# Two query heads take the first k tile beside the forget heads, and weight blocks are rounded behind chosen Exps

## The chip, the core and the metric

The kernel runs on one core of one Trainium2 chip. The metric is the device time of one execution in microseconds (us). Before the change three timed runs took 719.71 to 720.10 us, median 720.06 us.

Engine names are those of the profile: PE multiplies matrices, ACT does activations and copies, DVE does elementwise work, POOL (GpSimd) here fills constants and issues some transfers, SP only issues transfers. Every engine runs its own instructions strictly in the order in which they stand.

## The reference

One decoder layer over 512 positions of width 1024, in float32. What matters for this change is its beginning: the RMSNorm of x, and one projection whose columns are cut into heads.

```
h = rms_norm(x, norm_mix)
proj = h @ w_in
hq, hf, hi, hg, mq, mk, mv = split(proj, IN_SPLITS)
o_hgrn = hgrn2_mixer(hq, hf, hi, hg, lb, hgrn_norm)      # 4 heads of 128
#   f = lb + (1-lb) sigmoid(hf);  b = cumsum of log f inside chunks of 32
#   q_t = hq exp(b);  k_t = (1-f) exp(-b);  k_end = (1-f) exp(b_last - b)
#   o = causal(q_t k_t^T) hi + state part, then a norm and a gate from hg
o_moba = moba_attention(mq, mk, mv)
x = x + concat(o_hgrn, o_moba) @ w_out
```

Cross-attention into 256 memory tokens, a squared-ReLU MLP and a last RMSNorm follow. The change does not touch them.

## The kernel before

**Products in three parts.** Each float32 operand is split into a rounded high part and the rest (for a weight block: `wh` and `wl`, for x: `xhi` and `xlo`). A product is three matmuls: high by high, high by low, low by high. The high part of a weight block is made by an ACT copy (`split_raw`), the low part by a DVE subtraction right behind it. Blocks are numbered by use: 0 to 3 hold the forget heads (`hf`), 4 to 7 the values (`hi`), 8 to 11 the query heads (`hq`, one head each), 12 to 15 `mv`.

**Loading.** A block arrives in one of three raw buffers (`wr`). The load of block u, issued by SP, waits until the DVE subtraction of block u-3 has read the same buffer. `need(u)` is called before the matmuls of block u: it loads ahead as far as the three buffers allow and splits blocks up to u+2 (`SPLIT_AHEAD`). From block 8 on, each load also takes the next of a list of transfers between tensors in device memory (the tiles `m` and `u`, sums of weights for later stages); POOL issues most of them, and each waits for the matmul that stood last at the previous `need`.

**The first projection.** Four heads `hf` are accumulated over the eight k tiles of x, which arrive one by one. Before the first tile is there PE runs 11 small matmuls on a tile of ones (`warm`). The first block is loaded by heads: heads 0 and 1 and heads 2 and 3 of its first k tile come by two transfers from the ACT queue, the rest by SP. Beside this ACT and DVE sum the squares of x; two matmuls into the tile `nr` add them over partitions, just ahead of the last k tile, and ACT makes `rb` = 1/sqrt by a Ln and an Exp (`rsqrt_of`). Each change of function set costs an `ACT_TABLE_LOAD`.

**Forget gates and what follows.** `ev_f` multiplies each `hf` bank by `rb` (DVE), takes the sigmoid (ACT) and scales it (DVE), all into `Fz`. Then one ACT instruction takes the log of all four heads (`lnf`), and `hgrn_pre` works through the heads: a running sum `b` on DVE, three Exps on ACT (`eb`, `kt`, and the decay, in place in `lnf`), and some twenty DVE instructions that end in `ke`. Meanwhile PE does the values `hi` (`tm_stage`: four banks, four blocks) and then the query heads. When a query head is complete, `ev_q` scales its bank on DVE into `qx` (two halves, each with products by `dc` and `ee`) and `q4`. The attention part of the head, `hgrn_out`, is woven into the matmuls of the next heads: transposes of `ke` (`ket`), then 28 small matmuls into a bank `a` that need `qx`.

**What sets the order.** Up to the last k tile of `hf` the order is the written one. After it a scheduler orders each engine's instructions by its own estimates; the interleaving of side work into the matmul stream goes by a table of costs (`Pace`). All instructions carry the line of the recording helper, 118, so the profile is read by tile names.

## Time and profile before

| what | value |
|---|---|
| timed runs, median of 3 (lowest, highest) | 720.06 us (719.71, 720.10) |
| profiled execution: its span, the only time that its page gives | 717.5 us |
| PE busy | 709.5 us, 99% of the span |
| DVE busy | 580.7 us, 81% |
| ACT busy | 451.8 us, 63% |
| POOL busy | 81.1 us, 11% |
| moved by DMA | 155.58 MB, mean 217 GB/s |

The span runs from the first instruction to the last of one profiled execution. "Busy" is the time in which an engine had work; a busy share near 100% says that the engine bounds the kernel unless its own instructions are stretched. A row of the timeline gives the start and the length of a run of like instructions, and in brackets how long the engine sat idle before them and what released it. Tile names have their buffer numbers left out, so `wh` stands for any rounded weight block.

### The profile page before, as it was taken

Reading aid. Unit: us, or ns where it says so; the run is one execution under the profiler, and the core shown is the slowest. Engines: PE = TensorE matmul, PEld = TensorE weight load, DVE = VectorE, ACT = ScalarE, POOL = GpSimd, SP = SyncE. Lnnn points to the kernel's source line nnn. Section 1 sums busy time; section 2 is a strip of 40 time slices with the busy share of each in tenths; the row PEclk is TensorE's granted clock in tenths of the full one; section 3 lists DMA queues with packets and bytes.
Section 4 is the critical chain, followed back from the end, with each engine's and each line's share of the span. In section 5 each row is a group of like instructions: output and inputs, shape, how many; then the busy total and the mean of one; then the engine's idle time right before and its main releaser. Section 6 shows DMA issues by size and latency. Waiting matters only on the chain.

```text
span 717.5 us, 10748 instructions
## 1 busy us (share of the span) xinstructions
PE 709.5 (99%) x4038; PEld 613.2 (85%) x4038; DVE 580.7 (81%) x882; ACT 451.8 (63%) x654; POOL 81.1 (11%) x98
## 2 busy tenths in 40 slices
PE   9999999999999999999999999999999999999996
PEld 7888888888888888888888999999999888888885
DVE  6899537898787777777578889989899999987886
ACT  7884585546586677656565865566657655546672
POOL 2511132000000000002201111011110100110000
PEclk9999999999999999999999999999999999999999
DMA  8999689975556856458986587886898965998523
GB/s 295 274 281 318 166 175 253 368 257 144 156 173 195 249 175 202 148 177 200 267 266 156 139 225 197 223 206 193 218 233 258 288 220 192 276 276 252 177 89 117
DMA packets 62531, 155.58 MB, mean 217 GB/s; under 512 B 5232, under 2 KB 19184, under 8 KB 61968
## 3 DMA queue, kind: packets, MB, share of 16 engines
q1 hardware_dynamic: 47008, 116.43, 46.3%
q0 software_dynamic: 14592, 37.75, 28.7%
q10 hardware_dynamic: 880, 0.72, 0.3%
q8 instruction: 31, 0.51, 0.3%
q14 instruction: 20, 0.16, 0.1%
HBM read 152.79 MB, written 48.23 MB: 280 GB/s over the span
## 4 chain that ended last, share of the span: by engine, by line
PE 98%; DMA 1%; ACT 0%; DVE 0%; DVEq 0%; SPq 0%; issue 0%; ACTq 0%
PE Y L118 16%; PE X L118 12%; PE xo L118 8%; PE XB L118 6%; PE XA L118 6%; PE mkq L118 6%; PE xq L118 6%; PE wo L118 6%; PE mv L118 3%; PE hg L118 3%; PE hq L118 3%; PE Z L118 3%; PE hf L118 3%; PE memX L118 3%; PE hi L118 3%; PE memY L118 2%
## 5 line engine op out<-in xcount | busy, mean ns | idle before, releaser
L118 DVE TENSOR_TENSOR wl<-wr,wh 128x1024 fp32r<-128x1024 f32 (+2 forms) x139 | 165.6, 1196 | 33.8 <-ACT wh L118 27.1
L118 ACT ACTIVATE wh<-wr 128x1024 fp32r<-128x1024 f32 (+2 forms) x139 | 142.8, 1036 | 75.0 <-PE X L118 16.3
L240 POOL DMA_DIRECT2D u<-in_ws_dram x32 | 27.4, 874 | 320.9 <-PE xt L118 87.7
L118 PE MATMUL X<-op,wh 128*128 128x512 f32 (+1 forms) x264 | 62.9, 385 | 0.0
L118 PEld LDWEIGHTS X<-op,wh 128*128 128x128 f32 x264 | 47.2, 189 | 8.5
L118 PE MATMUL Y<-op,wh 128*128 128x512 f32 x192 | 47.2, 391 | 0.0
L118 PEld LDWEIGHTS Y<-op,wh 128*128 128x128 f32 x192 | 35.0, 189 | 6.6
L118 PEld LDWEIGHTS X<-op,wl 128*128 128x128 f32 x256 | 33.5, 191 | 1.6
L118 PE MATMUL X<-op,wl 128*128 128x256 f32 x256 | 34.1, 282 | 0.0
L118 PE MATMUL Y<-OS,wh 128*128 128x256 f32 x256 | 33.4, 283 | 0.0
L118 PEld LDWEIGHTS Y<-OS,wh 128*128 128x128 f32 x256 | 32.5, 192 | 0.7
L118 DVE TENSOR_TENSOR op<-g,op 128x1024 fp32r<-128x1024 f32 x24 | 29.3, 1219 | 2.8 <-ACT op L118 2.8
L118 ACT ACTIVATE op<-g 128x1024 fp32r<-128x1024 f32 x28 | 29.3, 1045 | 0.6 <-PE XB L118 0.6
L118 ACT ACT_TABLE_LOAD x20 | 25.7, 1283 | 2.2 <-issue 1.8
L118 PEld LDWEIGHTS Y<-op,wl 128*128 128x128 f32 x192 | 25.3, 191 | 1.3
L118 PE MATMUL Y<-op,wl 128*128 128x256 f32 x192 | 25.7, 282 | 0.0
L118 PE MATMUL xq<-x1hi,wl 128*128 128x512 f32 x64 | 25.6, 399 | 0.0
L118 PE MATMUL mkq<-xhi,wh 128*128 128x512 f32 x64 | 25.4, 397 | 0.0
L118 PE MATMUL mkq<-xhi,wl 128*128 128x512 f32 x64 | 25.4, 397 | 0.0
L118 DVE TENSOR_TENSOR wl<-wD,wh 128x1024 fp32r<-128x1024 f32 x15 | 18.4, 1224 | 8.6 <-ACT wh L118 7.9
L118 PE MATMUL xq<-x1hi,wh 128*128 128x512 f32 x64 | 25.3, 396 | 0.0
L118 PE MATMUL mkq<-xlo,wh 128*128 128x512 f32 x64 | 25.2, 394 | 0.0
(370 smaller groups left out, 1914.0 us busy)
## 6 DMA issues: line engine op xcount, KB each, us to landing
wr<-in_ws_dram SPq DMA_DIRECT2D x87, 512.0 KB, 5.0
u<-in_ws_dram POOLq DMA_DIRECT2D x32, 512.0 KB, 6.8
wr<-u SPq DMA_DIRECT2D x32, 512.0 KB, 4.4
u<-in_ws_dram SPq DMA_DIRECT2D x16, 512.0 KB, 11.9
wr<-m SPq DMA_DIRECT2D x16, 512.0 KB, 3.5
m<-in_ws_dram POOLq DMA_DIRECT2D x12, 512.0 KB, 9.8
m<-in_ws_dram POOLq DMA_DIRECT2D x16, 256.0 KB, 6.0
wA<-in_ws_dram SPq DMA_DIRECT2D x8, 512.0 KB, 5.1
```

Source lines behind the costliest of these rows:

```text
L118: return f(*args, **kw)
L240: return nc.gpsimd.dma_start(dst, src, accum_op=ALU.add, max_dma_last_dim=4 * D)
```

## The change

Six things are done.

1. Two query heads (blocks 8 and 9) get their first k tile (128 of 1024 rows) through tiles of their own: one transfer of 128 KB into `qr`, an ACT copy into `qh`, a DVE subtraction into `ql`, and six matmuls right behind those of the four forget heads on k tile 0. Later these two heads start at k tile 1. The number of matmuls stays.
2. `warm` has 8 matmuls and not 11. Heads 2 and 3 of the first weight tile are loaded by SP behind the first x tile, no longer from the ACT queue; `qr` follows them, ahead of the second x tile.
3. The two query banks are taken from the pool `acc` at the start, so the first two banks of `hi` come from the pool of side banks.
4. Weight blocks 5 and 6 are rounded on ACT behind the first Exp of `rsqrt_of`; at k tile 6 `need` splits one block less ahead.
5. Block 12, the first of `mv`, is rounded behind the Exp of the last head's decay; the preparation of the last head (`hgrn_pre`) is drained before the last two query heads.
6. The call order of `ev_f` is heads 2, 0, 1, 3.

```
-    GAP, SLACK, WARM = 4, 2.5, 11
+    GAP, SLACK, WARM = 4, 2.5, 8
...
     def split_raw(u, raw, a, b, eng=None):
-        A.activation(his[u][:, a:b], raw[:, a:b], AF.Copy)
+        rounded = A.activation(his[u][:, a:b], raw[:, a:b], AF.Copy)
+        if u in (5, 6):
+            tc.add_manual_dep(rounded.ins, first_root[0].ins.name, BEHIND)
+        elif u == W_MV:
+            tc.add_manual_dep(rounded.ins, last_decay[0].ins.name, BEHIND)
...
-    def need(u):
+    def need(u, ahead=SPLIT_AHEAD):
...
-        want_load, want_split = min(last, u + LOAD_AHEAD + 1), min(last, u + SPLIT_AHEAD + 1)
+        want_load, want_split = min(last, u + LOAD_AHEAD + 1), min(last, u + ahead + 1)
...
+    W_HQ, QE = 8, 2
+    q_raw, q_hi, q_lo = (s2(d, n)[:, :QE * P] for d, n in ((F32, "qr"), (F32R, "qh"), (F32R, "ql")))
     SY.dma_start(vec, vecs)
     load_x(0)
     load_first(0, 0, slice(0, 2), A)
-    load_first(0, 0, slice(2, 4), A)
+    load_first(0, 0, slice(2, 4))
+    SY.dma_start(q_raw.rearrange("p (n c) -> p n c", n=QE), ws[W_HQ:W_HQ + QE, :, :P].rearrange("n p c -> p n c"))
     load_x(1)
...
     split_first(0, 0, slice(2, 4))
+    A.activation(q_hi, q_raw, AF.Copy)
+    V.tensor_sub(q_lo, q_raw, q_hi.bitcast(F32))
...
-        A.activation(dst, dst, AF.Exp, scale=-0.5)
+        first_root.append(A.activation(dst, dst, AF.Exp, scale=-0.5))
...
+    q_accs = [acc_bank(f"hq{j}") for j in range(QE)]
...
-            need(k // 2)
+            need(k // 2, SPLIT_AHEAD - (k == KT - 2))
...
+        if k == 0:
+            cols = [slice(n * P, (n + 1) * P) for n in range(QE)]
+            for acc, c in zip(q_accs, cols):
+                mm(acc, q_hi[:, c], a_hi, True, False)
+            for acc, c in zip(q_accs, cols):
+                mm(acc, q_lo[:, c], a_hi, False, False)
+            for acc, c in zip(q_accs, cols):
+                mm(acc, q_hi[:, c], a_lo, False, False)
-    for h in range(HEADS):
+    for h in (2, 0, 1, 3):
         ev_f(h, accs[h])
...
-        A.activation(lf, lf, AF.Exp)
+        last_decay[0] = A.activation(lf, lf, AF.Exp)
...
-    tm_stage(u, x_act, 4, ev_hi, "hi")
+    tm_stage(u, x_act, 4, ev_hi, "hi", beside=(0, 1))
...
-    fm_stage(u, x_act, T, ev_q, "hq", ONE * 4)
+    for n in range(QE):
+        need(u + n)
+        for k in range(1, KT):
+            fm_k(u + n, q_accs[n], x_act, k, False, k == KT - 1)
+        ev_q(n, q_accs[n])
+    drain(("pre", HEADS - 1))
+    fm_stage(u + QE, x_act, T, lambda n, acc: ev_q(n + QE, acc), "hq", ONE * (4 - QE))
```

The order of the instructions moves at three places that matter below. The rows name the operation, what it writes and reads with buffer numbers, and the shape.

SP's queue from its start, before:

```order
L118 DMA vec_112<-in_vecs_dram 128x52
L118 DMA xraw0_122<-in_xT_dram 128x512 x2
L118 DMA wr0_130<-in_ws_dram 128x4x128
L118 DMA xraw0_122<-in_xT_dram 128x512
L118 DMA wr1_136<-in_ws_dram 128x4x256
```

And in the change:

```order
L118 DMA vec_112<-in_vecs_dram 128x52
L118 DMA xraw0_122<-in_xT_dram 128x512
L118 DMA wr0_133<-in_ws_dram 128x2x128
L118 DMA qr_128<-in_ws_dram 128x2x128
L118 DMA xraw0_122<-in_xT_dram 128x512
L118 DMA wr0_133<-in_ws_dram 128x4x128
L118 DMA xraw0_122<-in_xT_dram 128x512
```

Two transfers of 128 KB now stand between the first and the second tile of x (`xraw0`); the first of the two came from ACT's queue before.

ACT around the first reciprocal root (`rb1`), before:

```order
L118 ACTIVATE wh4_309<-wr4_255 128x1024
L118 ACTIVATE wh5_339<-wr5_257 128x1024
L118 ACTIVATE wh6_406<-wr6_259 128x1024
L118 ACTIVATE rb1_242<-nr_250,eps_118 128x512
L118 ACT_TABLE_LOAD
L118 ACTIVATE rb1_242<-rb1_242 128x512
L118 ACTIVATE lbv_245<-lbv_245 128x8
L118 ACT_TABLE_LOAD
L118 ACTIVATE Fz_244<-Fz_244 128x512 x4
L118 ACTIVATE wh7_461<-wr7_313 128x1024
L118 ACT_TABLE_LOAD
L118 ACTIVATE lnf_400<-Fz_244 128x2048
```

And in the change:

```order
L118 ACTIVATE wh4_320<-wr4_260 128x1024
L118 ACTIVATE rb1_245<-nr_255,eps_118 128x512
L118 ACT_TABLE_LOAD
L118 ACTIVATE rb1_245<-rb1_245 128x512
L118 ACTIVATE lbv_248<-lbv_248 128x8
L118 ACTIVATE wh5_407<-wr5_262 128x1024
L118 ACT_TABLE_LOAD
L118 ACTIVATE Fz_247<-Fz_247 128x512 x4
L118 ACTIVATE wh6_417<-wr6_264 128x1024
L118 ACTIVATE wh7_472<-wr7_324 128x1024
L118 ACT_TABLE_LOAD
L118 ACTIVATE lnf_401<-Fz_247 128x2048
```

The roundings of blocks 5 and 6 moved from ahead of the root to between it and the log `lnf`; the next rounding, of block 8, stands right behind `lnf` in both.

DVE behind the forget banks, before:

```order
L118 TENSOR_TENSOR Fz_244<-hf3_249,rb1_242 128x512
L118 TENSOR_SCALAR lbv_245<-lbv_245 128x4
L118 TENSOR_TENSOR own_430<-rb1_242,ident_121 128x512
L118 TENSOR_SCALAR Fz_244<-Fz_244,lbv_245 128x512 x4
L118 TENSOR_REDUCE rc1_243<-own_430 128x4
L118 TENSOR_TENSOR wl7_462<-wr7_313,wh7_461 128x1024
```

And in the change:

```order
L118 TENSOR_TENSOR Fz_247<-hf3_252,rb1_245 128x512
L118 TENSOR_SCALAR lbv_248<-lbv_248 128x4
L118 TENSOR_TENSOR wl5_408<-wr5_262,wh5_407 128x1024
L118 TENSOR_SCALAR Fz_247<-Fz_247,lbv_248 128x512 x4
L118 TENSOR_TENSOR wl6_418<-wr6_264,wh6_417 128x1024
L118 TENSOR_TENSOR own_441<-rb1_245,ident_121 128x512
L118 TENSOR_TENSOR wl7_473<-wr7_324,wh7_472 128x1024
```

The subtractions `wl5` and `wl6`, which set free the raw buffers of the loads of blocks 8 and 9, moved behind the products of `hf` with `rb1`. In both programs SP's queue has the loads of blocks 8, 9 and 10 in a row, each waiting for such a subtraction. One more pair of DVE rows changed places: `qx0` of head 1 (`hq1`) now stands between the first product of `qx1` of head 0 and the two that finish it. On PE, apart from the six matmuls and the three of `warm`, nothing moved. POOL's rows stand as before, but the first four transfers into `m0_0` wait for the end of k tile 5 where they waited for that of k tile 3, since the load of block 8 that brings them is written one `need` later.

More of the change, by code (lines that the diff above doesn't have):

```diff
@@ L301, in hybrid_layer @@
     AFTER = mybir.DependencyInfo(mybir.DependencyClass.Sync, mybir.DependencyReason.DATA)
+    BEHIND = mybir.DependencyInfo(mybir.DependencyClass.NoSync, mybir.DependencyReason.SCHED_ONLY)
     marks = [None]
@@ L331, in sums_after @@
         return u % 2 == 0 and (4 <= u - FF2 < 14 or u - FF2 >= 26)
-    held = []
+    W_MV = 12
+    held, first_root, last_decay = [], [], [None]
     def later(f):
@@ L516, in fm_stage, with tm_stage @@
             u += size
-    def tm_stage(u0, act, ntok, evac, name):
-        accs = [acc_bank(f"{name}{t}") for t in range(ntok)]
+    def tm_stage(u0, act, ntok, evac, name, beside=()):
+        accs = [(side_bank if t in beside else acc_bank)(f"{name}{t}") for t in range(ntok)]
         for j in range(4):
@@ L873, in ev_q @@
         start(hgrn_out(h, qx, q4), ("out", h))
-    fm_stage(u, x_act, T, ev_q, "hq", ONE * 4)
+    assert u == W_HQ
+    for n in range(QE):
[5 more added lines that the diff above has]
+    fm_stage(u + QE, x_act, T, lambda n, acc: ev_q(n + QE, acc), "hq", ONE * (4 - QE))
     u += 4
```

## The prediction

> **What bounds the kernel now.** I read the busy shares of the page first:
>
> ```profile
> PE 709.5 (99%) x4038; PEld 613.2 (85%) x4038; DVE 580.7 (81%) x882; ACT 451.8 (63%) x654; POOL 81.1 (11%) x98
> ```
>
> Then all waits of PE (us in total, times, longest):
>
> ```profile
> PE warm L118 <- POOL eps L592: 1.0, 1, 1.0
> PE hf L118 <- ACT xhi L118: 0.3, 1, 0.3
> ```
>
> Then the beginning of the chain of work that ended last (start, us, what), and a window at the end of the span (stretch, width, busy time and count of PE, PEld, DVE, ACT and POOL, granted clock, DMA share, GB/s):
>
> ```profile
> 1.19 3.74 DMA xraw<-in_xT_dram
> 5.57 19.36 PE hf L118 x84
> ```
>
> ```profile
> 710.90:714.20 3.30, 0.00 (x0) 0.00 (x0) 2.04 (x4) 0.97 (x4) 1.41 (x2) 1.00 0.47 170
> ```
>
> PE is busy 99% of the 717.5 us span and waits twice in all, both times before its first `hf` at 5.57. From there it is filled to 710.9, where the last matmul is behind it. This decides how everything below counts. Other engines cost nothing by being busy; a delay anywhere counts only if it opens a gap on PE, and such a gap then passes whole to the end. A gain can come only from an earlier first `hf`, since the matmuls behind it stay the same in number: six of them are only moved forward.
>
> How much earlier it can be, by two rows of the timeline, a window, and two DMA issues with their us to landing:
>
> ```profile
> 0.99 4.29 PE L118 MATMUL warm<-ones 128*128 128x128 f32 x22 [0.99 <-POOL eps L592]
> 5.01 0.51 ACT L118 ACTIVATE xhi<-xraw,vec 128x256 fp32r<-128x256 f32 x1 [1.31 <-DMA xraw<-in_xT_dram]
> ```
>
> ```profile
> 0.99:4.30 3.31, 3.31 (x15) 3.31 (x16) 0.43 (x1) 1.90 (x3) 2.96 (x10) 1.00 0.69 169
> ```
>
> ```profile
> xraw<-in_xT_dram SPq DMA_DIRECT2D x1, 256.0 KB, 3.7
> wr<-in_ws_dram ACTq DMA_DIRECT2D x1, 128.0 KB, 2.5
> ```
>
> The 11 `warm` matmuls are 22 rows; 15 rows took 3.31 us, so 8 matmuls (16 rows) end near 4.5 and leave room for at most 1.0 us. The matmul waits for `xhi`, and `xhi` for the first x tile, which took 3.7 us from its issue at 1.19.
>
> **The change, part by part.**
>
> *Start.* The second transfer of ACT's queue, 128 KB, ran beside the x tile and now follows it. Without any sharing, a tile of 256 KB must take longer than the 2.5 us that 128 KB took; the added 128 KB cost 0.4 us at the 338 GB/s of the window 45:60 that is quoted below (an estimate). So landing lies between 2.9 us (gain 0.8) and 3.7 (no gain). I take 3.1, since the second transfer started last and overlapped only in part: **gain g = 0.6 us**, bounds 0 and 1.0. The six matmuls cost 6 x 0.23 us (19.36/84) = 1.4 us here and save the same later: 0 in the sum. They are also the cover for the 256 KB that now arrive ahead of the second x tile (0.8 us at the same rate, of which half came beside it before; against 1.4 - g = 0.8 us of added PE work). ACT's copy `qh` and DVE's `ql` (128x256 like the `xhi` row, 0.5 us each) lie beside PE's twelve matmuls on tile 0; without that cover they would cost up to 1.0 us.
>
> *The log of the gates comes later.* PE's last matmul into `nr`, and ACT's rows around the first root:
>
> ```profile
> 25.01 0.40 PE L118 MATMUL nr<-nrl,ones_r 128*128 128x512 f32 x1
> ```
>
> ```profile
> 22.98 3.03 ACT L118 ACTIVATE wh<-wr 128x1024 fp32r<-128x1024 f32 x3
> 25.91 0.67 ACT L118 ACTIVATE rb<-nr,eps 128x512 f32<-128x512 f32 x1
> ...
> 32.91 1.06 ACT L118 ACTIVATE wh<-wr 128x1024 fp32r<-128x1024 f32 x1 [0.78 <-DMA wr<-in_ws_dram]
> ...
> 35.29 1.92 ACT L118 ACTIVATE lnf<-Fz 128x2048 f32<-128x2048 f32 x1
> 37.11 1.04 ACT L118 ACTIVATE wh<-wr 128x1024 fp32r<-128x1024 f32 x1
> 38.06 0.61 ACT L118 ACTIVATE Fz<-Fz 128x512 f32<-128x512 f32 x1
> ```
>
> Before, the root's Ln stood behind three roundings, at 25.91. Now two of them are gone from there, but `nr` is later by the six matmuls: 25.41 + 1.4 - 0.6 = 26.2, so the root starts 0.3 later, not earlier. Then `wh5` and `wh6` (one every 0.95 us: 37.11 to 38.06) stand between root and `lnf`: +1.9. The 0.78 us in which ACT waited for block 7 are swallowed: -0.78. Together `lnf` comes **1.4 us later**, at 36.7.
>
> *Where that lag goes.* DVE's rows behind `lnf` and at the end of its chain, a window between them, and the PE row that reads the result:
>
> ```profile
> 45.00:60.00 15.00, 15.00 (x68) 12.40 (x67) 14.99 (x40) 9.42 (x15) 5.95 (x8) 1.00 0.98 338
> ```
>
> ```profile
> 37.31 2.34 DVE L118 TENSOR_TENSOR_SCAN b<-scan_mask,lnf 128x512 f32<-128x512 f32 x2 [1.83 <-ACT lnf L118]
> ...
> 63.54 0.41 DVE L118 TENSOR_TENSOR qx<-hq,eb 128x256 f32<-128x256 f32 x1
> 63.99 0.29 DVE L118 TENSOR_TENSOR qx<-qx,dc 128x128 f32<-128x128 f32 x1
> 64.20 0.22 DVE L118 TENSOR_TENSOR qx<-qx,ee 128x64 f32<-128x64 f32 x1
> ```
>
> ```profile
> 65.93 0.25 PE L118 MATMUL a<-qx,Fz 128*32 128x96 f32 x1
> ```
>
> DVE waits 1.83 us for `lnf`, then works without a gap: 14.99 of 15 us between 45 and 60. A lag at 37 us therefore is still there at 64 us. The second half of `qx` of the first head is finished at 64.42; PE's first matmul that reads it starts at 65.93, so there are 1.5 us of slack. PE is g earlier, DVE 1.4 later, and the moved `qx0` of the next head puts some 0.2 us more (63.54 to 63.99 less what overlaps) ahead of the last two. Stall: 0.6 + 1.4 + 0.2 - 1.5 = **0.7 us**. Bounds: 0, if DVE's small gaps take up the lag or PE reaches `a` later, and 1.2. Since a larger g makes the lag of `lnf` smaller by as much, this stall hardly depends on g.
>
> *Block 8 comes later still.* This is the term that decides the sign. SP's load of block 8 waits for `wl5`. DVE's rows at its old and its new place, three answers on loads of 512 KB with their us to landing (issued around 15, between 24 and 40, and at 35.5 us), a window, and the DMA queues between 37 and 39 us:
>
> ```profile
> 24.06 2.36 DVE L118 TENSOR_TENSOR wl<-wr,wh 128x1024 fp32r<-128x1024 f32 x2 [0.26 <-ACT wh L118]
> ...
> 31.24 0.68 DVE L118 TENSOR_TENSOR own<-rb,ident 128x512 f32<-128x512 f32 x1
> ```
>
> ```profile
> wr<-in_ws_dram SPq DMA_DIRECT2D x1, 512.0 KB, 3.6
> ```
>
> ```profile
> wr<-in_ws_dram SPq DMA_DIRECT2D x4, 512.0 KB, 7.7
> ```
>
> ```profile
> wr<-in_ws_dram SPq DMA_DIRECT2D x1, 512.0 KB, 7.5
> ```
>
> ```profile
> 33.00:39.00 6.00, 6.00 (x28) 4.98 (x27) 4.17 (x6) 5.95 (x6) 2.28 (x2) 1.00 1.12 221
> ```
>
> ```profile
> q0 software_dynamic: 211, 0.40, 109.6%
> ...
> q1 hardware_dynamic: 1, 0.00, 0.5%
> ```
>
> Before, `wl5` was the second of the two rows at 24.06 and ended at 26.4. Now it stands where `own` stood, 31.24 + 0.3, and takes 1.2: it ends near 32.7, and the load is issued 6.3 us later than before. Its rounding `wh8` stands right behind `lnf` on ACT and could start at 37.11 + 1.4 = 38.5. So the load may take 5.8 us. The load around 15 us had SP's queue alone (3.6); the four between 24 and 40 have a median of 7.7; the one issued at 35.5, the nearest in time, took 7.5. Between 33 and 39 us the DMA engines are full (share 1.12) with POOL's transfers in device memory; from 37 to 39 the rows give POOL's queue q0 109.6% and SP's q1 0.5%, although a load was pending. And the stretch gets fuller: of the eight transfers below, POOL issued the first four at 17.09, and these now wait for a later k tile like the others.
>
> ```profile
> 17.09 3.21 POOL L269 DMA_DIRECT2D m<-in_ws_dram  x4 [12.93 <-PE hf L118]
> 22.50 2.94 POOL L269 DMA_DIRECT2D m<-in_ws_dram  x4 [2.20 <-PE hf L118]
> ```
>
> I take 7.5: block 8 lands at 40.2 to 40.3 and `wh8` is **1.8 us late**. Bounds: 0 at 3.6 us of latency, 3.7 at 9.5 us. Behind `wh8` on ACT stand the last gate scaling, a table load and the Exps that DVE's chain needs next, so this lag goes the way of the first, into the wait of `a`: +1.8, with no slack left to take it. Blocks 9 and 10 are issued some 8 and 3 us later too, but their roundings stood at 43.65 and 45.63, which leaves them over 8 us each: 0 by the same latency.
>
> The Trainium skill says in "DMA: Bandwidth & Descriptors", section "Queues, rings and completion order", that each DMA engine goes round robin between the queue rows that have work, packet by packet. By that rule SP's queue gets a share as soon as it has work, and this speaks against the last term. The trace does not agree in the 37 to 39 us window, where q1 had next to nothing.
>
> *The rest.* The order of `ev_f`, block 12 behind the last decay, and the swapped banks move ACT and DVE work between 66 and 85 us that has PE work beside it; PE's waits are unchanged there: 0. The granted clock stays at 1.00 in the 3.3 us after the last matmul (row 710.90), so a stall of 1 to 3 us costs its own length.
>
> **Sum**: -0.6 + 0.7 + 1.8 = **+1.9 us**. The profiled execution would go from 717.5 to 719.4; the median of the timed runs, 720.06, is 2.6 above that span, and I keep that difference: **722.0 us**.
>
> **The rivals.**
>
> *A: block 8 lands in time.* If SP's queue gets its turn among POOL's transfers, the load needs half the full rate, between 3.6 and 5.8 us. This is the round robin just named. Then W = 0 and the sum is -0.6 + 0.7 = +0.1: 720.2 us. For it: all loads between 24 and 40 did land, in 7.5 to 9.5 us, with the engines full. Against it: none was as fast as 5.8.
>
> *B, the other side: PE is not stalled at all, and g survives.* The place is PE's first `a` with the second half of `qx`. If block 8 is in time and DVE regains 0.7 us of its lag, so that this half is ready when PE gets there, only the start is left: 719.4 (719.1 with g = 1.0). For it: DVE gives up `wl5` and `wl6` from its order ahead of the 1.83 us in which it waited for `lnf`, and a scheduler may have left small gaps between 37 and 45 us. Against it: that idle time lay ahead of the chain, not in it, and 14.99 of 15 us leave nothing to regain.
>
> *C: the first `hf` run at the slow pace.* The `warm` rows ran 15 in 3.31 us, then the last 7 in 0.98 us (to 5.28), so PE became faster near 4.3, though the window has the granted clock at 1.00. With `warm` ending at 4.5 and a pause behind it, the pace could fall again; if `hf` loses what `warm` lost (3.31 - 15 x 0.14 = 1.2 us), 723.2. Against it: the 0.3 us pause of before left no trace.
>
> *D: the lag cascades.* Latency 9.5 us and block 9 late too: +3.7 + 0.1 = 723.9.
>
> **How the numbers follow.** A difference of 0.2%, 1.4 us, is about what a measurement of this kernel can tell from no change. Forecast (block 8 late by 0.5 to 3 us) 0.58; A 0.22; B 0.06; C 0.03; D 0.07; and 0.04 for something missed on the faster side, since the start alone can give 1.0 us and not 1.4. Of the forecast 0.40 lies above +1.4 us (a latency of 7.1 us and more), 0.18 below. Slower by over 0.2%: 0.40 + 0.03 + 0.07 = 0.50. Within 0.2%: 0.18 + 0.22 + 0.06 = 0.46. Faster: 0.04. The range reaches from B, 719.3, to 723.5, just below D; the forecast alone would be 720.7 to 723.2.
>
> **What the changed profile would show.** The first `hf` near 5.0 (not 5.57) and `xhi` near 4.4: g. The log `lnf` near 36.7. Block 8's load issued near 32.7, with 7 to 8 us to landing, and ACT idle some 1.8 us before the rounding behind `lnf`, released by a DMA. In PE's waits a new row of about 2.5 us, `a` waiting for `qx` of DVE near 65, and the last matmul near 712.8. If that row is missing, B; if it is 0.7, A. A latency near 4 us, or `lnf` at its old place, would make the prediction wrong, as would a gap on PE anywhere else.

## The result, and the profile after

The changed kernel takes 728.92 us (median of 4 runs, 727.88 to 730.02), the kernel before 719.88 us in the same comparison. The ratio is 1.0128 with a 95% interval of 1.0114 to 1.0142: **9 us slower**. The forecast was 722.0 us, range 719.3 to 723.5. The direction was right and the size was not: the time lies 5.4 us above the range.

The profiled execution has a span of 726.8 us (717.5 before), so 9.3 us are to be found. First the busy shares of its page, and all waits of PE:

```profile
PE 712.0 (98%) x4032; PEld 614.2 (85%) x4032; DVE 581.3 (80%) x883; ACT 452.1 (62%) x655; POOL 81.1 (11%) x98
```

```profile
PE a L118 <- DVE qx L118: 6.5, 1, 6.5
PE warm L118 <- POOL eps L601: 1.0, 1, 1.0
```

One wait of 6.5 us stands where none was. It is the wait that the prediction named (PE's bank `a` for `qx`), but it was to last 2.5 us. The rows around it tell why. DVE between 63 and 73 us, ACT's row at the same time, and one row of the chain of waits:

```profile
63.55 0.42 DVE L118 TENSOR_TENSOR qx<-hq,eb 128x256 f32<-128x256 f32 x1
70.17 1.23 DVE L118 TENSOR_TENSOR wl<-wr,wh 128x1024 fp32r<-128x1024 f32 x1 [6.20 <-ACT wh L118]
71.32 0.29 DVE L118 TENSOR_TENSOR qx<-qx,dc 128x128 f32<-128x128 f32 x1
```

```profile
69.09 1.06 ACT L118 ACTIVATE wh<-wr 128x1024 fp32r<-128x1024 f32 x1 [7.86 <-DMA wr<-in_ws_dram]
```

```profile
51.10 17.88 DMA wr<-in_ws_dram
```

Read them from the bottom. The load of block 12, the first of `mv`, was issued at 51.10 and took 17.9 us. ACT could round it only at 69.09. DVE's subtraction `wl12` waited for that, 6.2 us, and it stands in the middle of the first head's `qx`: ahead of it the first product (63.55), behind it the product with `dc` (71.32) that PE's bank `a` needs.

Before the change the order on DVE was the same. DVE's rows there, the load of block 12 with its us to landing, and PE's first matmul that reads block 12 itself:

```profile
61.40 0.42 DVE L118 TENSOR_TENSOR qx<-hq,eb 128x256 f32<-128x256 f32 x1
61.73 1.21 DVE L118 TENSOR_TENSOR wl<-wr,wh 128x1024 fp32r<-128x1024 f32 x1
62.87 0.28 DVE L118 TENSOR_TENSOR qx<-qx,dc 128x128 f32<-128x128 f32 x1
```

```profile
wr<-in_ws_dram SPq DMA_DIRECT2D x1, 512.0 KB, 8.0
```

```profile
77.75 0.39 PE L118 MATMUL mv<-wh,xhi 128*128 128x512 f32 x1
```

Block 12 was issued at 49.66 then and landed at 57.7, 4 us ahead of its subtraction. PE needs it only for `mv`, some 12 us of its work behind bank `a`; in the change PE stood still because of what was queued behind the block.

The rest of the loss is the clock. Windows of the changed kernel (stretch, width, busy and count of PE, PEld, DVE, ACT, POOL, granted clock, DMA share, GB/s):

```profile
65.00:69.00 4.00, 0.32 (x8) 0.05 (x7) 0.00 (x0) 0.00 (x0) 0.00 (x0) 1.00 0.56 222
69.00:72.00 3.00, 0.21 (x8) 0.21 (x12) 1.83 (x5) 2.49 (x3) 0.00 (x0) 0.61 0.05 22
72.00:76.00 4.00, 3.99 (x53) 2.90 (x47) 4.00 (x14) 0.00 (x0) 0.00 (x0) 0.50 0.80 277
```

After PE had stood idle from 65.3 to 71.8 it worked on at a granted clock of 0.50 (1.2 GHz) until 76: four us of work at half speed. Comparing the start of the same matmuls in both traces gives the whole account: at the end of `hf` the new start had gained 0.5 us; at bank `a` and behind it PE lost 9.2, of which 6.5 are the wait; after that the lag stays at 8.65 us to the last matmul. Another 0.6 us lie behind the last matmul (below, at the stores).

Why was block 12 late? The DMA engines from 20 to 26 and from 26 to 60 us, first before and then after the change:

```profile
20.00:26.00 6.00, 6.00 (x28) 4.92 (x27) 4.80 (x7) 3.56 (x5) 3.25 (x5) 1.00 0.89 289
26.00:60.00 34.00, 34.00 (x152) 28.13 (x151) 31.11 (x86) 27.52 (x39) 10.63 (x12) 1.00 1.01 295
```

```profile
20.00:26.00 6.00, 6.00 (x28) 4.97 (x27) 4.80 (x8) 2.04 (x3) 2.61 (x4) 1.00 0.41 132
26.00:60.00 34.00, 34.00 (x152) 28.09 (x151) 30.25 (x76) 27.86 (x38) 14.16 (x17) 1.00 1.01 284
```

Their share falls from 0.89 to 0.41 there: 0.48 of 6 us, 2.9 us of all engines are not used, since POOL's first four copies now go out at 23.39 and not at 17.09 (e1 below, which has them early again, has 0.88). From 26 to 60 us the engines are full (1.01 in both), so there is no free time in which to catch this up. And the loads of blocks 8 and 9 are themselves issued 6.5 and 8.6 us later than before, because `wl5` and `wl6` moved. Which of the two matters, and how, the experiments had to tell.

### The profile page after: what moved, and what is told of

Read it like the earlier page. It is cut to its first block, busy times and chain, and to the rows that moved or that the text cites. A ratio compares the mean times of both kernels' runs of the same rounds, so it can differ in the third digit from the quotient of the medians.

```text
span 726.8 us, 10736 instructions
## 1 busy us (share of the span) xinstructions
PE 712.0 (98%) x4032; PEld 614.2 (85%) x4032; DVE 581.3 (80%) x883; ACT 452.1 (62%) x655; POOL 81.1 (11%) x98
## 4 chain that ended last, share of the span: by engine, by line
PE 93%; DMA 4%; DVE 2%; ACT 1%; issue 0%; DVEq 0%; POOL 0%; ACTq 0%; POOLq 0%
PE Y L118 16%; PE X L118 12%; PE xo L118 8%; PE XB L118 6%; PE XA L118 6%; PE mkq L118 6%; PE xq L118 6%; PE wo L118 6%; DMA wr<-in_ws_dram 4%; PE mv L118 3%; PE hg L118 3%; PE Z L118 3%; PE memX L118 3%; PE hf L118 3%; PE memY L118 2%; PE xs L118 2%
## 5 line engine op out<-in xcount | busy, mean ns | idle before, releaser
L118 PE MATMUL xq<-x1lo,wh 128*128 128x512 f32 x64 | 25.2, 393 | 0.0
```

Of the source, the lines that this page charges most:

```text
L118: return f(*args, **kw)
```

## The experiments

Times are medians beside the kernel before on the same chip (719.6 to 719.8 us in all of them). "Lag" is how much later than before the change the last matmul stands in the profiled execution; for the changed kernel it is 8.6 us. Kernels in which PE waits for late blocks scatter by 2 to 8 us between executions, and a profile shows one of these, so for them it says more on the mechanism than on the size.

| kernel | median us | ratio to before, 95% | lag us |
|---|---|---|---|
| the change | 728.92 | 1.0128 (1.0114 to 1.0142) | 8.6 |
| e1 copies early again | 725.31 | 1.0078 (1.0061 to 1.0095) | 3.5 |
| e2 copies late alone | 719.59 | 1.0007 (0.9996 to 1.0018) | 1.3 |
| e6 rounding late alone | 720.95 | 1.0016 (1.0007 to 1.0025) | 0.7 |
| e8 only block 6 late | 720.93 | 1.0015 (1.0006 to 1.0023) | 0.5 |
| e7 `m3` copies later | 721.35 | 1.0023 (1.0014 to 1.0033) | 0.5 |
| e3 `wl12` behind `qx` | 727.55 | 1.0106 (1.0077 to 1.0135) | 7.3 |
| e4 block 12 free | 729.96 | 1.0145 (1.0129 to 1.0160) | 8.6 |
| e14 blocks 12, 13 last | 723.79 | 1.0062 (1.0042 to 1.0081) | 2.6 |
| e12 filled, wrong place | 731.03 | 1.0154 (1.0122 to 1.0186) | 7.8 |
| e13 filled ahead of `a` | 726.25 | 1.0092 (1.0076 to 1.0107) | 6.9 |
| e5 start alone | 720.42 | 1.0010 (1.0002 to 1.0019) | 0.6 |
| e10 start without query tile | 721.20 | 1.0024 (1.0015 to 1.0033) | 2.1 |
| e9 one more transfer | 719.93 | 1.0000 (0.9992 to 1.0009) | 0.2 |
| e11 best put together | 719.96 | 1.0007 (0.9998 to 1.0016) | 0.1 |

### Two causes: late copies, late loads

e1 takes the changed kernel and calls the first four copies early again:

```
     def load_unit():
-        for _ in range(sums_after(u)):
+        for _ in range(sums_after(u) if u != W_HQ else 0):
             more_sums()
...
             need(k // 2, SPLIT_AHEAD - (k == KT - 2))
+            if k == KT - 2:
+                more_sums()
+                more_sums()
```

> The changed kernel, with one thing undone: the first four copies of POOL into m0 are again called at k tile 6 and so wait for the end of k tile 3 (they went out at 17.09 us before the change and at 23.39 us after it); the load of block 8 and all rounding stay where the change put them. Theory 1 (the late copies leave the DMA engines idle between 20 and 26 us, share 0.58 against 0.86 over 20 to 30, and the 1 MB that is missing then is paid back out of the loads of blocks 11 to 14): block 12 lands near 58 to 60 us as before (57.7) and not at 69.0, PE waits at most 0.7 us for qx, 719 to 720.5 us. Theory 2 (the loads of blocks 8 to 10 are issued 6.5, 8.6 and 2.5 us later because wl5 and wl6 moved, and this is the backlog): block 12 lands at 65 us or later, PE still waits 3 us or more, 724 us or more.

Measured: 725.3 us. Block 12 was issued at 53.9 and took 10.0 us, landing at 63.9, between the two theories; the time is in theory 2's range. The profiled execution is the fastest of the six (723.4; the slowest took 727.8), and in it block 12 no longer held anything. What PE waited for now was the other lag, the one that the prediction had put in its sum, in ACT's rows behind `lnf` (here at 37.08) and PE's waits:

```profile
41.34 1.06 ACT L118 ACTIVATE wh<-wr 128x1024 fp32r<-128x1024 f32 x1 [2.33 <-DMA wr<-in_ws_dram]
```

```profile
PE a L118 <- DVE qx L118: 2.1, 3, 1.0
```

Block 8, issued at 33.27, took 8.0 us, its rounding waited 2.33 us behind `lnf`, DVE was dense from there (10.00 of 10 us busy between 50 and 60) and PE waited at bank `a` in three pieces. With the copies early this execution does what the prediction said; what made the others up to 4.4 us slower no profile shows. With the copies late, as the change has them, block 8 meets DMA engines that are less full (a share of 0.91 from 33 to 38 us, 1.08 in e1) and takes 5.0 us; the time is lost at block 12.

e2 is the kernel before with those four copies late and nothing else, e6 the kernel before with the rounding of blocks 5 and 6 behind the root and the copies at their old time:

```
 e2, on the kernel before
-        for _ in range(sums_after(u)):
+        for _ in range(sums_after(u) if u != 8 else 0):
...
     def need(u):
+        if u == 4:
+            more_sums()
+            more_sums()
```

> The kernel before, with this one thing of the change alone: the first four copies into m0 are called one need later, so they wait for the end of k tile 5 and are issued near 22.5 us together with the next four. No instruction of PE, ACT, DVE or SP moves. Theory 1: the DMA engines are idle for some 3 us between 17 and 22 us, blocks 11 and 12 land 3 to 8 us later than 52.4 and 57.7 us, the DVE subtraction wl12 (at 61.7 us before) holds qx, PE waits 1 to 5 us for qx, 721 to 726 us. Theory 2: no new wait on PE, 719.7 to 720.3 us.

```
 e6, on the kernel before
-        for _ in range(sums_after(u)):
+        for _ in range(sums_after(u) if u != 8 else 0):
...
+        if u in (5, 6):
+            tc.add_manual_dep(rounded.ins, first_root[0].ins.name, BEHIND)
...
-            need(k // 2)
+            need(k // 2, SPLIT_AHEAD - (k == KT - 2))
+            if k == KT - 2:
+                more_sums()
+                more_sums()
```

> The kernel before with part 4 of the change alone (blocks 5 and 6 rounded behind the first root's Exp), the first copies of POOL kept at their old time and the old start. Theory (the load of block 8 is issued 6 us later and the full DMA engines then take 7 to 8 us for it, as the run with early copies showed: issued 33.3, landed 41.3): the load is issued near 32, lands near 40, its rounding is 2 us late, lnf 0.7 us late, together 2.9 us against 1.5 us of slack, so PE waits 1.2 to 1.8 us for qx near 65 us: 721.0 to 722.0 us. Rival (the loss needs the late copies or the new start): PE waits under 0.5 us, 719.5 to 720.3 us.

e2 measured 719.59 us, no difference in the median. But four of its ten executions took 720.6 to 723.0 us, more than any of the 23 of the kernel before beside it (719.0 to 720.1), and the profiled one is among the four. It shows theory 1's chain, in small: the copies alone delay block 12 (issued 50.59, 12.7 us, landed at 63.3 instead of 57.7), and DVE waits for its rounding:

```profile
64.46 1.23 DVE L118 TENSOR_TENSOR wl<-wr,wh 128x1024 fp32r<-128x1024 f32 x1 [1.72 <-ACT wh L118]
```

PE's waits have no row behind its first `hf`, but in small gaps at bank `a` it loses 1.1 us. So theory 2 holds for the median, and theory 1 at least for the profiled execution. e6 measured 720.95 us, 1.2 us slower, just under the expected 721.0. Its profile shows the expected chain, smaller:

```profile
39.29 1.06 ACT L118 ACTIVATE wh<-wr 128x1024 fp32r<-128x1024 f32 x1 [1.70 <-DMA wr<-in_ws_dram]
```

The load of block 8 was issued at 31.86 and took 7.3 us; PE's lag grew by 0.9 us at bank `a`.

So block 12 lands at 57.7 with neither cause, at 60.6 with late loads alone (e6), at 63.3 with late copies alone (e2), at 63.9 with late loads and the new start (e1), and at 69.0 with all three. The new start alone gives 59.4 (e5, below). The single delays, 2.9, 5.6 and 1.7 us, make 10.2 of the 11.3; with one profile each this is rough, and five other kernels with all three land it between 65.2 (e12) and 68.7 us. The slack is small: DVE did not wait for the block in e1 and e6, where it landed at 63.9 and 60.6 and DVE was late itself, and waited 1.7 us in e2 and 6.2 in the change. That is why neither half shows the whole loss.

e8 removes both at once, with one line less: only block 6 goes behind the root, so block 5's subtraction frees the buffer for block 8 early, and no `need` has to split less ahead.

```
-        if u in (5, 6):
+        if u == 6:
...
-            need(k // 2, SPLIT_AHEAD - (k == KT - 2))
+            need(k // 2)
```

> The changed kernel with only block 6 rounded behind the root; block 5 stays ahead of it, so its subtraction frees the raw buffer for the load of block 8 near 27.5 us as before, and no need splits one block less, so POOL's first copies keep their old time. Theory: both causes are gone at once; blocks 8 and 12 land near 34 and 58 us, the values no longer wait for the forget banks (0.6 us in the run with the start alone), lnf is about 1 us late within 1.5 us of slack: no wait of PE over 0.3 us behind the first hf, the last matmul 0.3 to 0.6 us earlier than before, and with the 0.65 us that the stores at the end took longer in all runs with the new start, 719.3 to 720.2 us. Rival: the moved rounding of block 6 makes blocks 9 and 12 late instead, PE waits over 1 us, 721 us or more.

Measured 720.93 us, above the expected 719.3 to 720.2, but 8 us better than the change. Block 12 took 7.2 us and landed at 57.3, the values did not wait, and up to 543 us PE ran 0.5 us ahead of the kernel before, as expected. Then it lost 1.0 us at one place of the MLP, in a part that the change does not touch:

```profile
DVE wd L118 <- DMA wd<-in_ws_dram: 2.9, 1, 2.9
...
PE XB L118 <- DVE g L118: 0.7, 1, 0.7
```

The same wait is in the profiles of e1, e3 and e10 and in none of the others. Why it comes and goes was not followed.

### The debt belongs to all transfers of the stretch

e7 leaves everything of the change and only calls POOL's eight copies into `m3` (2 MB, 51 to 58 us) with later loads:

```
-            return 2 * (u >= 8) + (u >= 22)
+            return 2 * (8 <= u < 14 or u >= 16) + (18 <= u < 22) + (u >= 22)
```

> The changed kernel, with the eight copies of POOL into m3 (2 MB, issued at 51 to 58 us) called with later weight loads, so that they run behind 70 us; all else as changed. Theory (a debt of DMA work: 1 MB not moved between 20 and 26 us is taken from the last loads in SP's queue because POOL's m3 copies, issued on their own marks, go beside them): block 12 lands by 62 us and not at 69.0, PE waits at most 1 us for qx (its chain is still 1.4 us late): 720.0 to 721.5 us. Rival (block 12 is late by what stands before it in SP's own queue, the m2 copies, or by single lagging DMA engines): it lands at 66 us or later, PE waits 3 us or more, 724 us or more.

Measured 721.35 us, in the expected range. Block 12 took 10.8 us from 51.33 and landed at 62.1, and of the 6.5 us wait this is left:

```profile
PE a L118 <- DVE qx L118: 0.2, 1, 0.2
```

Nothing that was late in the change is earlier here: the copies into `m0` still go out at 23.19, block 8 at 32.70. 2 MB out of the way of SP's queue undo most of the loss, so it is beside these copies that block 12 loses most of its time. (Four transfers of SP, `m1` from `m0`, move later too; they stood behind block 12.) The second half of the rival, single lagging DMA engines, is not excluded by this; the last section comes back to it.

### It reaches PE through what is queued behind the late block

```
 e3, on the change: wl12 behind the last product of the first head's qx
+            if u == W_MV:
+                tc.add_manual_dep(low.ins, last_qx[0].ins.name, BEHIND)
...

 e4, on the change: no order for block 12
-        elif u == W_MV:
-            tc.add_manual_dep(rounded.ins, last_decay[0].ins.name, BEHIND)
```

> The changed kernel, with DVE's subtraction of block 12 (wl12) ordered behind all of the first query head's qx instead of between its first and second product; the loads and copies stay late. If wl12, waiting for the late block 12, is what holds qx (both theories on the backlog agree here): PE no longer waits at 65 us; wl12 now holds the qx of the second head, whose bank a PE reached at 70.1 us by its order, until about 72.5, so PE waits about 2 to 2.5 us there, the granted clock falls less or not at all, 721 to 723 us. Rival: the first head's qx is late for another reason (its own chain behind lnf, 1.4 us later plus what follows), then PE still waits at the first a for more than 2 us, 724 us or more.

> The changed kernel without part 5's order for block 12 (its rounding may stand ahead of the last head's decay, where ACT's order then puts it). Theory (block 12 is late in device memory traffic, whatever its place on ACT): ACT and DVE still wait for it with qx queued behind, and the last head's decay and ke now too; 728 to 731 us. Rival (the place behind the last decay is what made block 12 and so qx late): 721 to 724 us.

e4 measured 729.96 us, as the theory said: block 12's place behind the last decay is not the cause (PE waited 6.1 us at the same place). e3 measured 727.55 us and was a miss. The wait at `a` is gone but for 0.6 us, as expected; the delay found another queue. On ACT the copy `kets` of the first head stands behind the roundings of blocks 12 and 13, and PE's `pd` needs it:

```profile
PE pd L118 <- ACT kets L118: 1.6, 1, 1.6
```

Behind that wait (PE idle from 69.8 to 71.4) the granted clock was 0.50 until 75:

```profile
72.00:74.00 2.00, 2.00 (x8) 1.71 (x7) 2.00 (x5) 0.53 (x2) 0.00 (x0) 0.50 0.93 280
```

The lag grew from 2.1 to 3.9 us over the wait, to 5.6 at the lower clock, and by another 1.7 at the place of the MLP named at e8. So 3.5 of the 7.3 us are this queue and its clock, and 1.7 come from a wait far behind it.

e14 therefore takes everything of the attention out from behind both blocks, on both engines:

```
+        ahead -= u == W_MV - 2
...
-        elif u == W_MV:
-            tc.add_manual_dep(rounded.ins, last_decay[0].ins.name, BEHIND)
+        elif u in (W_MV, W_MV + 1):
+            tc.add_manual_dep(rounded.ins, (kets.get(0) or last_decay[0]).ins.name, BEHIND)
...
+            if u in (W_MV, W_MV + 1):
+                tc.add_manual_dep(low.ins, last_qx[1].ins.name, BEHIND)
```

> The changed kernel, with the loads and copies as late as it has them, but nothing of the attention queued behind blocks 12 and 13: their roundings on ACT stand behind the first head's kets, their subtractions on DVE behind the second head's qx (block 12 is split one need later for that, and the load of block 15 with its copies is called one need later). Theory (late blocks cost only through what stands behind them in the queues of ACT and DVE): block 12 still lands at 65 us or later, PE waits at most 0.7 us for qx and at most 1 us for kets or S: 720.0 to 722.0 us. Rival (PE is held by the gate chain itself or by the weights): PE waits 3 us or more between 64 and 80 us, 724 us or more.

Measured 723.79 us (722.09 to 726.07), between the two expectations; the profiled execution has a span of 720.8. Block 12 is as late as in the change (16.2 us from 51.72, landed at 67.9), ACT waits for it, and PE hardly does:

```profile
67.96 1.06 ACT L118 ACTIVATE wh<-wr 128x1024 fp32r<-128x1024 f32 x1 [2.93 <-DMA wr<-in_ws_dram]
```

```profile
PE a L118 <- DVE qx L118: 1.2, 1, 1.2
```

5 of the 9 us come back with the block still late. What is left is DVE's chain for `qx`, which block 11 holds now: its rounding waited 3.4 us for its load and DVE 1.6 us for the rounding. The other five executions took from 0.5 us less to 3.5 us more than this one, so the last step to the old time is not shown.

### The price of the clock

```
 e12, on the change
         for t in range(NT):
             q = qx[t // 2][:, t % 2]...
+            for i in range(22 if (h, t) == (0, 2) else 0):
+                nc.tensor.matmul(pa[:, t * P:(t + 1) * P], ones, ones, start=True, stop=True, ...)

 e13, on the change
         pa = side_bank("a")
+        for i in range(22 if h == 0 else 0):
+            nc.tensor.matmul(pa[:, :P], ones, ones, start=True, stop=True, ...)
         for t in range(NT):
```

> The changed kernel, with 22 small matmuls on the tile of ones put ahead of the first matmul that needs the second half of the first head's qx, that is into the 6.5 us in which PE stood still (they write columns of bank a that the real matmuls then overwrite). Of the 9.2 us that PE lost there, 6.5 are the wait and 2.7 are left; the granted clock was 0.50 from 70 to 76 us. Theory: the 2.7 us are the price of the lower clock after the idle time; with PE busy (5 to 6 us of small matmuls) the clock stays at 1.00 and the kernel gets 2 to 3 us faster though it does more: 726.0 to 727.0 us. Rival: the rest of the loss is later waits for DVE and the transfers, and the clock only goes with it: 728.3 to 729.5 us, or more.

> The changed kernel with the 22 small matmuls on the tile of ones put ahead of the whole bank a of the first head, in front of the place where PE stood still (the run that put them ahead of the third tile of the bank had them behind the wait, where they only cost their 5.2 us). Theory (2 to 2.7 of the 9.2 us lost are the lower clock after the idle time): the small matmuls fill 5.2 of the 6.5 us, the rest is waited for, the granted clock stays at 1.00 from 65 to 80 us, PE loses 6.5 to 7 us there and not 9.2: 726 to 727.3 us. Rival (the clock costs nothing of its own): 728.3 to 730 us.

e12 was a badly made experiment. It put the small matmuls ahead of the third tile of bank `a`, where the second half of `qx` is needed; but PE stood still for the first half, so they ran behind the wait and only cost their own length:

```profile
67.97 0.27 PE L118 MATMUL a<-qx,Fz 128*32 128x96 f32 x3 [1.48 <-DVE qx L118]
68.48 5.18 PE L836 MATMUL a<-ones 128*128 128x128 f32 x44
```

It tells nothing on the clock (731.0 us). It does show how much the late block varies: up to the wait the program is that of the change, but in this execution (727.05, the fastest of four by 4 us) block 12 landed at 65.2 and DVE waited 1.9 us for it, not 6.2. e13 has them in front of the bank, in the wait (row of PE, then windows):

```profile
65.37 5.08 PE L834 MATMUL a<-ones 128*128 128x128 f32 x44
```

```profile
65.00:70.00 5.00, 5.00 (x46) 4.95 (x45) 0.44 (x2) 1.06 (x1) 0.00 (x0) 1.00 0.53 210
70.00:75.00 5.00, 3.99 (x72) 2.83 (x70) 5.00 (x14) 1.82 (x3) 0.00 (x0) 1.00 0.55 162
```

726.25 us, as expected: 22 matmuls more, block 12 as late as ever (17.0 us), and 2.7 us faster, with a granted clock of 1.00 throughout. In the profile PE loses 6.9 us at the bank and not 9.2. So some 2.5 of the 9 us were the clock (2.3 by the profiles, 2.7 by the medians), the rest the wait. The executions of either kernel lie up to 2 us apart, so this size is rough.

### The start

e5 has the new start alone (parts 1 to 3), e10 only its 8 `warm` matmuls and the moved transfer, with no query tile:

```
 e5, on the change
-        if u in (5, 6): ... elif u == W_MV: ...
-            need(k // 2, SPLIT_AHEAD - (k == KT - 2))
+            need(k // 2)
-    for h in (2, 0, 1, 3):
+    for h in range(HEADS):
-    drain(("pre", HEADS - 1))

 e10, on the kernel before
-    load_first(0, 0, slice(2, 4), A)
+    load_first(0, 0, slice(2, 4))
-    GAP, SLACK, WARM = 4, 2.5, 11
+    GAP, SLACK, WARM = 4, 2.5, 8
```

> The start of the change alone (parts 1 to 3: two query heads take k tile 0, 8 warm matmuls, the transfer behind the first x tile), with the rounding of blocks 5, 6 and 12, the ahead count at k tile 6, the order of ev_f and the drains as before. Theory 1 and 2 both: the first hf stays at 4.8 us as in the changed kernel, no new wait on PE, so 720.06 - 0.8 = 719.2 us (719.0 to 719.6). Rival (the six moved matmuls make nr, the root and with it the whole gate chain 0.6 us later, with 1.5 us of slack at a): PE waits for qx after all, 719.6 us or more.

> The kernel before with only two things of the new start: 8 warm matmuls, and heads 2 and 3 of the first weight tile loaded by SP behind the first x tile; no query heads beside k tile 0, no new tiles. The first hf should come at 4.8 us as with the whole start. If the six moved matmuls are the cover for the later second x tile, PE now waits 0.3 to 0.8 us for it and the last matmul is 0 to 0.5 us earlier than before; if they are not needed as cover, 0.7 to 0.8 us earlier. On the stores at the end (85 ns per packet before, 98 with the new start): 98 ns if the transfer that moved from ACT's queue to SP's makes it, 85 ns if the transfer of the query tile does. So 719.0 to 719.9 us with 85 ns, 719.6 to 720.5 with 98.

e5: 720.42 us, the gain is not there. The first `hf` is at 4.80 as expected, and `hf` ends 0.6 us ahead of its old pace; but a wait that no theory had named takes it back:

```profile
PE hi L118 <- DVE Fz L118: 0.6, 1, 0.6
```

The third bank of the values takes over a bank of `hf`, which DVE can give free only with `rb`; and the root still stands behind the rounding of block 6, whose load landed at 27.8 us (24.8 before), so DVE's first product with `rb` starts at 31.51 and not at 28.56. PE loses 0.9 us there and 0.3 more at bank `a`. Moving roundings behind the root takes this wait away (it is in no profile that has part 4 or e8's half of it), and it is what spoils the loads; e8 shows that one block is enough. What the new call order of `ev_f` (part 6) did is not shown: the profile's rows leave the bank numbers out.

e10: 721.20 us, slower. PE's rows at its first two k tiles:

```profile
5.67 0.73 PE L118 MATMUL hf<-xhi,wh 128*128 128x512 f32 x2 [0.90 <-ACT xhi L118]
...
9.04 0.50 PE L118 MATMUL hf<-xhi,wh 128*128 128x512 f32 x1 [0.35 <-ACT wh L118]
```

The six moved matmuls are needed as cover, as expected: without them PE waits for the second k tile, and `hf` ends 1.3 us late. (The other 0.8 us of e10's lag are the wait in the MLP named at e8.) The first row was not expected: the first x tile came no earlier than before, although the transfer that shared its time is away. Its load took 3.8 us here (3.7 before the change), and in the changed kernel

```profile
xraw<-in_xT_dram SPq DMA_DIRECT2D x1, 256.0 KB, 2.9
```

In that stretch of SP's queue the two differ by the query tile's transfer, which holds back the issue of the second x tile from 2.12 to 2.63 us. So it seems to be the second x tile that the first one shares its time with, more than the 128 KB that moved. The other profiles agree: the first x tile took 2.9 to 3.4 us in the eleven with the query tile, and 3.4 to 3.7 in the four with the old start, where the second tile is issued at 1.65. No run changes the second tile's issue alone, so this is argued, not shown.

### The stores at the end, and the best version

```
 e9, on the kernel before
     for k in range(5, KT):
         load_x(k)
+    spare = s2(F32, "spare")
+    SY.dma_start(spare[:, :52], vecs)
```

> The kernel before with one more small load from device memory (26 KB into a tile that nothing reads), behind the x tiles in SP's queue. It asks why the stores at the end land 0.65 us later behind the last matmul in every run with the new start (one transfer more) and not in the two without. If the number of transfers decides (it shifts the order in which the queues and their semaphores are used): the packets of the last stores take 98 ns and not 85, the end comes 0.65 us later, 720.2 to 720.5 us. If not: 719.5 to 719.9 us and 85 ns.

719.93 us: the number of transfers is not it. Behind the last matmul 6.7 us are left in some profiles and 7.3 in others, and the rows of the last stores differ alike (before, then e5):

```profile
out_dram<-g SPq DMA_DIRECT2D x3, 256.0 KB, 2.9
```

```profile
out_dram<-g SPq DMA_DIRECT2D x3, 256.0 KB, 3.5
```

It is not the new start either: e12 and e13 have it and end in 6.6 us, e10 has no query tile and ends in 7.4. The cause stays open; 0.6 us of any one profile here hang on it. In the traces the 2 KB packets behind the last matmul took 86 ns on the mean before and 98 in e5, with a median of 84 in both, so a part of the packets is slower and not all.

e11 joins e8 and e7.

> The best of the runs so far put together: the changed kernel with only block 6 rounded behind the root (block 5 ahead of it, POOL's first copies at their old time) and POOL's copies into m3 called with later loads. Theory: no wait of PE behind the first hf up to 500 us, the last matmul 0.5 us earlier than before the change; the stores at the end are at 85 or at 97 ns per packet (0.5 to 0.65 us apart), so 719.2 to 720.5 us, between no change and 0.1% better than before. Rival: the later m3 copies collide with the loads of a later stage, and PE waits over 0.5 us between 70 and 350 us: 720.8 us or more.

719.96 us, ratio 1.0007 (0.9998 to 1.0016): no wait of PE behind its first `hf`, and no gain. Its `hf` ended 0.1 us behind the old pace in the profiled execution. Over all profiles with the new start and the query tile, `hf` ends between 0.7 us ahead (e7) and 0.7 us behind (e12), 0.1 us ahead on the mean of eleven. The half us that the start is worth in the changed kernel's profile is not there in every execution. No version found beats the kernel before.

## Why the prediction was wrong, step by step

**What bounds the kernel.** Right: everything lost is lost in gaps of PE or in what follows one. Wrong in one half sentence: "a stall of 1 to 3 us costs its own length" was read from the 3.3 us behind the last matmul; the stall was 6.5 us long and cost 9.2, because the clock fell (some 2.5 us by e13). Nor did it hold for a stall of 1.6 us in e3: three us at a granted clock of 0.50 followed, in which another 1.7 us were lost.

**The start, 0.6 us.** The first `hf` came 0.8 us earlier, of which 0.5 were left at the end of `hf`. The size was right in this profile and is unsure over all of them (e11). The reason given, the moved 128 KB, is not enough for it (e10: the transfer moved, no gain). The cover by six matmuls was right.

**The log comes 1.4 us later, at 36.7.** Exact, by the row of ACT in the changed kernel:

```profile
36.72 1.92 ACT L118 ACTIVATE lnf<-Fz 128x2048 f32<-128x2048 f32 x1
38.54 1.04 ACT L118 ACTIVATE wh<-wr 128x1024 fp32r<-128x1024 f32 x1
```

**The stall of 0.7 us from that lag.** Not seen by itself under the 6.5 us. In e7, where block 12 is in time, PE loses 1.1 us at the bank.

**Block 8 is 1.8 us late.** The issue was right (32.7 forecast, 32.9 measured); the latency was not, in the changed kernel: 5.0 us and not 7.5. The row at 38.54 follows `lnf` without idle time. That is rival A for this block. In e1, with the copies early, the load took 8.0 us and the term was there at 2.3 us; in e6 at 1.7. Over the seven profiles with late copies and late loads it took 3.4 to 7.0 us. So that the time moved the way of the forecast was in part luck: the term that decided the sign was missing, and without it the sum was +0.1 us. The row of 7.5 us from which it was taken belonged to a stretch in which POOL's copies had already been issued early, and the change moves them. The round robin rule that the prediction weighed (the Trainium skill, "DMA: Bandwidth & Descriptors", section "Queues, rings and completion order") gives SP's queue its share as soon as it has work. At half the rate a load that took 3.6 us alone would need 7.2 (an estimate): 5.0 us agrees with the rule, 8.0 us in e1 is a little beyond it, and 17.9 us for block 12 far beyond.

**The failed step** is the one called "The rest": "The order of `ev_f`, block 12 behind the last decay, and the swapped banks move ACT and DVE work ... that has PE work beside it ... 0", together with "Blocks 9 and 10 ... 0". The late transfers were followed up to block 10 and no further, and block 12 was put at nothing for PE, although its subtraction stands inside `qx`; it measured a wait of 6.5 us and a loss of 9.2. The late copies were seen, and counted only as something in the way of block 8. What they are is DMA time that passes unused (2.9 us at 20 to 26 us) ahead of a stretch in which the DMA engines are full for 34 us. Here such a debt stayed until the loads at the end of that stretch (e2), and 2 MB less beside them paid most of it (e7). Why SP's loads pay and not POOL's copies is not shown. The trace of before had what was needed to see it: a DMA share of 1.01 from 26 to 60 us, 4 us between the landing of block 12 and its subtraction, and that subtraction standing inside `qx`.

**The rivals.** D, the cascade, was of the right kind ("block 9 late too", 0.07), but named the wrong block, and ended at 723.9.

**The baseline.** The 2.6 us between the median and the span mix two executions. In the records each execution's time is 1.8 us above its own span (728.57 and 726.8 for the change); this moves the forecast time by 0.8 us and not the forecast difference.

## What to carry to other kernels

Where the DMA engines are full over a long stretch, a transfer that is issued later can be a debt that comes due far from it: here not at the load of block 8 but at that of block 12. So follow the whole stretch to its end, and give every load in it its landing and its slack. Look at what stands behind a wait in the queue of its engine: a weight block that PE needs 12 us later stopped PE because its subtraction stood inside another chain. Two delays that slack mostly covers one by one can add up beyond it (medians: e2 0 us, e6 1.2 us, both with the new start 9 us), so changes that use up the same slack have to be costed together.

## What the runs showed of the hardware that was not expected

- A load of 512 KB took 3.6 us with SP's queue alone, up to 9.5 beside POOL's copies before the change (block 9), and 17.9 at worst. While PE and DVE stood still for that one, from 66 to 70 us, the DMA share was 0.34.

```profile
66.00:70.00 4.00, 0.00 (x0) 0.00 (x0) 0.00 (x0) 0.91 (x1) 0.00 (x0) 0.96 0.34 135
```

The trace marks the landing of a load in 16 parts. Of block 12, 11 parts had landed by 63.0 us and the other five came between 65.7 and 69.0; before the change the 11th came at 54.8 and the last at 57.7. So 8.2 of its 11.3 us are common to all parts, and 3.1 are a wider spread between them. Which engines lagged, and why, the trace does not show.
- A wait that PE fills with useless matmuls costs less than the same wait idle: e13 does 5.1 us of them and is 2.7 us faster than the change.
- The last stores took 2.9 or 3.5 us from issue to landing, in different builds, with no cause found.
